# A short-conv mixer on one core: product b of a chunk's two pairs by seven products of half size, and buffers as 2 KB pages

## The chip, the core and the metric

The kernel runs on one core of a Trainium2 chip. The metric is the device time of one launch in microseconds (us). PE is TensorE, DVE VectorE, ACT ScalarE, POOL GpSimd, and SP the engine whose queue issues the transfers.

## The reference

With DEPTH = 1 there is one layer, the gated short convolution. Its input is 1024 tokens of width 1024, its inner width is 2048.

```python
u = rms_norm(x, pre_norm)
z, bg, cg, v = split(u @ w_in, 4, axis=-1)          # w_in: 1024 x 8192
y = bg * causal_dwconv(cg * v, conv_w) * silu(z)    # 3 taps per channel
h = x + rms_norm(y @ w_out, post_norm)              # w_out: 2048 x 1024
```

All is float32.

## The kernel before, in words

The work on `u @ w_in` goes by chunks of 128 inner channels (16 chunks) and, in each, by two pairs of 128-channel columns of `w_in`: an even pair p = 2c (cg and v) and an odd pair p = 2c+1 (z and bg). A pair is a product of a 2 x 2 block matrix (two channel columns by two halves of the model width) with a 2 x 2 block matrix of `u` (two halves of the model width by two halves of the tokens). It is done with seven block products instead of eight, named a, b, c, e, d, f, g in the order in which `ORDER` runs them. The sums of weight blocks that some of them need are made on GpSimd in `add_s`, the sums of `u` once at the start.

Each block product is 128 channels by 512 inner by 512 tokens. Every operand is split into a high part (a cast on ScalarE) and the rest (a subtraction on VectorE), in `split`; `product` then issues, for each of four inner slices of 128, three matmuls over 512 columns: low weight by high u, high weight by low u, high by high. That is 12 matmuls to a product. Products a, c, d, g accumulate in one PSUM bank (px), e and f in another (pv), b in a third (py). `after` reads a bank after each product: `snap` copies it to SBUF on ScalarE after a, c and e; after b, d and f VectorE adds the bank to the copy.

After g of an even pair the convolution follows: VectorE multiplies into `gpad`, and `conv` does the first tap on ScalarE and two more on VectorE, each over all 1024 tokens. After g of the odd pair the chunk is gated, and its y is written to DRAM (`y_done`).

The engines run their queues in the order in which the code issues, since the schedule is by hand. Between products the loop over p puts in the work for later pairs: `split_w` and `add_s` for pair p+1, `fetch` of the weights of pair p+2 on SP, and sums for the output stage (`fetch_t`, `add_t` on `w_out`; `fetch_s`, `add_y` on y). The first chunk (pair 0 plain, pair 1 in seven products) is mixed with the norm and the transposes of x. The output stage multiplies y by `w_out` with seven block products too (`out_mm`), its operands fetched and split a unit at a time (`fetch_unit`, `split_unit`), and ends with the norm and the residual.

Buffers come from several pools: `raw` (16 KB tiles: weights of a pair, sums, fetched units), `wp` (8 and 4 KB tiles: split weights), `snp`, `tmp`.

Of the kernel before, what the change touches and what calls it, by code (L numbers as in the profile page):

```python
# [14 lines left out]
WARM = 14  # L15


@with_exitstack
def kernel(
# [16 lines left out]
    nc = tc.nc  # L36
# [22 lines left out]
    wp = ctx.enter_context(tc.tile_pool(name="wp", bufs=3))  # L59
    raw = ctx.enter_context(tc.tile_pool(name="raw", bufs=3))  # L60
# [5 lines left out]
    def bank(name):  # L66
        return psum.tile([P, HB], F32, tag="bank", name=name)

# [42 lines left out]
    raws, sums, wt = {}, {}, {}  # L111

    def fetch(p, rows=(0, 1)):
        if p >= len(PAIRS):
            return
        c, tys = PAIRS[p]
        if p not in raws:
            raws[p] = raw.tile([P, 2, NK, P], F32, tag="raw", name=f"raw_{p}")
        for n in rows:
            c0 = tys[n] * CI + c * P  # L120
            nc.sync.dma_start(raws[p][:, n], wiv[:, :, c0 : c0 + P])

    def add_s(p, part):

        if p >= len(PAIRS):
            return
        r = raws[p]
        a11, a12, a21, a22 = (flat(r[:, n, k * KH : (k + 1) * KH]) for n in (0, 1) for k in (0, 1))
        if part == 0:
            sums[p] = raw.tile([P, 4, HB], F32, tag="sum", name=f"sum_{p}", bufs=1)  # L130
        s = sums[p]
        if part == 0:
            nc.gpsimd.tensor_add(s[:, 1], a21, a22)  # L133
            nc.gpsimd.tensor_sub(s[:, 0], s[:, 1], a11)
        else:
            nc.gpsimd.tensor_sub(s[:, 2], a11, a21)  # L136
            nc.gpsimd.tensor_sub(s[:, 3], a12, s[:, 0])  # L137
# [5 lines left out]
    def split_w(p, part):  # L143

        if p >= len(PAIRS):
            return
        n = 2 * HB if part < 3 else HB
        tag = "w8" if part < 3 else "w4"
        if p == 1 and part == 1:
            t = raw.tile([P, 2, n], F32R, tag="raw", name=f"w{part}_{p}")  # L150
        else:
            t = wp.tile([P, 2, n], F32R, tag=tag, name=f"w{part}_{p}", bufs=3 if part < 3 else 2)
        if part == 0:
            src = flat(raws[p][:, 0])
        elif part == 3:
            src = flat(raws[p][:, 1, KH:])
        else:
            src = flat(sums[p][:, 2 * (part - 1) : 2 * part])
        split(src, t[:, 0], t[:, 1])
        wt[p, part] = t  # L160


    WHERE = {"a": (0, 0), "b": (0, HB), "c": (1, 0), "e": (1, HB), "d": (2, 0), "f": (2, HB), "g": (3, 0)}
# [12 lines left out]
    def product(p, i, ks=None):  # L176

        part, off = WHERE[i]
        w = wt[p, part]
# [5 lines left out]
        for k in range(KH) if ks is None else ks:  # L185
            hi = w[:, 0, off + k * P : off + (k + 1) * P]
            lo = w[:, 1, off + k * P : off + (k + 1) * P]
            last = k == KH - 1
            nc.tensor.matmul(ps, lo, UH[i][:, k], start=first and k == 0, stop=False, skip_group_check=True)  # L189
            nc.tensor.matmul(ps, hi, UL[i][:, k], start=False, stop=False, skip_group_check=True)  # L190
            nc.tensor.matmul(ps, hi, UH[i][:, k], start=False, stop=last, skip_group_check=True)  # L191
# [3 lines left out]
    def snap(p, i):  # L195
        t = snp.tile([P, HB], F32, tag="sn", name=f"sn{i}_{p}", bufs=5)
        nc.scalar.copy(t, banks[p, "v" if i == "e" else "x"])
        sn[p, i] = t
# [5 lines left out]
    def after(p, i):  # L204
# [9 lines left out]
        elif i == "c" and p % 2:  # L214
            nc.scalar.activation(sn[p, "a"], sn[p, "a"], AF.Silu)
# [13 lines left out]
        elif i == "g":  # L229
# [5 lines left out]
            else:  # L235
                nc.vector.tensor_mul(gpad[:, TAPS - 1 : TAPS - 1 + HB], x_, sn[p, "a"])
                conv(c)
# [8 lines left out]
    def fetch_s(c):  # L246

        if c >= CH:
            done[c] = done[c], raw.tile([P, 4, HB], F32, tag="raw", name=f"s_{c}")
            nc.sync.dma_start(flat(done[c][1][:, :2]), y_d[:, c - CH])  # L250

    def add_y(c):

        if c < CH:
            cv = done.pop(c)
            t = tmp.tile([P, HB], F32, tag="s3", name=f"s3_{c}")
            nc.vector.tensor_sub(t, cv[:, :HB], cv[:, HB:])
            nc.sync.dma_start(s_d[:, SK["d"], c], t)
        else:
            cv, t = done.pop(c)  # L260
            nc.vector.tensor_add(t[:, 1], t[:, 1], cv[:, HB:])
            nc.vector.tensor_sub(t[:, 0], t[:, 1], t[:, 0])
            nc.vector.tensor_sub(t[:, 2], cv[:, :HB], t[:, 0])
            nc.sync.dma_start(s_d[:, :3, c - CH], t[:, :3])
# [3 lines left out]
    def fetch_t(j):  # L268
        ts[j] = raw.tile([P, 4, HB], F32, tag="raw", name=f"t_{j}")
        nc.sync.dma_start(ts[j].rearrange("p (k e) d -> p k (e d)", k=2), wov[:, j :: CH])  # L270

    def add_t(j, eng):

        t = ts.pop(j)
        eng.tensor_sub(t[:, 1], t[:, 1], t[:, 0])
        eng.tensor_sub(t[:, 3], t[:, 3], t[:, 1])
        eng.tensor_sub(t[:, 0], t[:, 3], t[:, 0])
        eng.tensor_sub(t[:, 2], t[:, 2], t[:, 3])
        nc.sync.dma_start(t_d[:, :, j], t)
# [8 lines left out]
    snp = mixed.enter_context(tc.tile_pool(name="snp", bufs=1, reuse_waits="tile"))  # L288
# [8 lines left out]
    rows = wp.tile([P, 2 + TH, P], F32, tag="w4", name="rows", bufs=2)  # L297
    grow, cw_rows = rows[:NK, 0], rows[: TAPS * NC, 1]
    junk = wp.tile([P, D], F32, tag="w4", name="junk", bufs=2)
    sq = small.tile([P, NT], F32, tag="sq", name="sq", bufs=1)  # L300
    gcol = small.tile([P, NK], F32, tag="gcol", name="gcol", bufs=1)
    dg = rows[:, 2:]
# [7 lines left out]
    raws[0] = raw.tile([P, 2, NK, P], F32, tag="raw", name="raw_0")  # L310
# [9 lines left out]
    def square(t):  # L320

        out = flat(raws[0][:, 0]) if t == 0 else junk
# [43 lines left out]
    def high_plain(p, n):  # L366
        plain_w[p, n] = wp.tile([P, 2, D], F32R, tag="w8", name=f"wn{n}_{p}", bufs=3)
        nc.scalar.copy(plain_w[p, n][:, 0], flat(raws[p][:, n]))

    def low_plain(p, n):  # L370
        t = plain_w[p, n]
        nc.vector.tensor_sub(t[:, 1], flat(raws[p][:, n]), t[:, 0].bitcast(F32))

    def plain(p, n, half, part, kks=range(4), first=None, last=None):
# [4 lines left out]
        ps, w = banks[p, n, half], plain_w[p, n]  # L379
        first = part == 0 if first is None else first  # L380
        last = part == 1 if last is None else last
        for j, kk in enumerate(kks):
            k = part * KH + kk
            hi, lo = (w[:, h, k * P : (k + 1) * P] for h in (0, 1))
# [5 lines left out]
    def plain_snap(p, n):  # L390
        t = snp.tile([P, HB], F32, tag="sn", name=f"sp{n}_{p}", bufs=5)
# [15 lines left out]
    for t in range(TH):  # L407
        square(t)
        if t == 0:
# [5 lines left out]
            fetch(2)  # L415
# [25 lines left out]
    low_plain(0, 1)  # L441
    for k in range(KH):
# [15 lines left out]
    split_w(1, 0)  # L458
# [11 lines left out]
    add_s(1, 0)  # L470
    rebuild(0, [2, 3])
    add_s(1, 1)
# [31 lines left out]
    sn[1, "a"] = snp.tile([P, HB], F32, tag="sn", name="sna_1", bufs=5)  # L504
# [13 lines left out]
    split_w(1, 1)  # L518
# [27 lines left out]
    split_w(1, 2)  # L546
# [8 lines left out]
    split_w(1, 3)  # L555
# [4 lines left out]
    split_w(2, 0)  # L560
# [8 lines left out]
    add_s(2, 0)  # L569
    add_s(2, 1)  # L570
    fetch(3)

    def conv(c):
        cv = tmp.tile([P, L], F32, tag="cv", name=f"cv_{c}", bufs=2)
# [7 lines left out]
    def first_chunk(i):  # L582

        if i == "":
# [4 lines left out]
            split_w(2, 1)  # L589
            conv(0)  # L590
            nc.gpsimd.tensor_mul(cvs[0][:, HB:], cvs[0][:, HB:], sn[1, "e"])
        elif i == "a":
            split_w(2, 2)
        elif i == "b":
            split_w(2, 3)
# [5 lines left out]
        elif i == "d":  # L601
# [3 lines left out]
            y_done(0, cv)  # L605

# [7 lines left out]
    def fetch_unit():  # L614
# [12 lines left out]
        tag, bufs = ("sum", 1) if n % 4 == 3 else ("raw", 3)  # L627
        r = raw.tile([P, CQ, HB], F32, tag=tag, name=f"r{side}_{i}{h}", bufs=bufs)
        nc.sync.dma_start(r, src)
        fetched.append(r)  # L630

    def split_unit():
# [5 lines left out]
        for q in (slice(0, CQ // 2), slice(CQ // 2, CQ)):  # L638
            split(flat(fetched[n][:, q]), flat(t[:, 0, q]), flat(t[:, 1, q]))
# [4 lines left out]
    TODO[2 * CH + 1] = CH - 1  # L644
    first_chunk("")
    for p in range(2, len(PAIRS)):
        q, prev = p + 1, p // 2 - 1
        for i in ORDER:
            product(p, i)
            after(p, i)  # L650
            if p == 2:
                first_chunk(i)
            if i == "a" and p < END:
                add_s(q, 0)
                if p in TODO:
                    fetch_t(TODO[p])
                if p % 2 == 0 and p > 2:
                    fetch_s(prev)
                if p + 2 <= END:
                    fetch(p + 2)  # L660
            if p == END - 1 and i in "cd":
                fetch_unit()
            if p == END:
                if i in "abcdg":
                    split_unit()
                    fetch_unit()
            elif i == "b":
                split_w(q, 0)
                add_s(q, 1)
                if p in TODO:  # L670
                    add_t(TODO[p], nc.gpsimd if p % 2 else nc.vector)
                if p == 3 or p % 2 == 0 and p > 2:
                    add_y(prev)
            elif i == ("e" if p > 2 else "d"):
                split_w(q, 1)
            elif i == "f":
                split_w(q, 2)
            elif i == "g":
                split_w(q, 3)
# [9 lines left out]
    gpost = wp.tile([P, D], F32, tag="w4", name="gpost", bufs=2)  # L689
    nc.sync.dma_start(gpost, post_norm.broadcast_to([P, D]))  # L690
    xr = wp.tile([P, 2, D], F32, tag="w8", name="xr", bufs=3)
    gx = wp.tile([P, TH, HB], F32, tag="w8", name="gx", bufs=3)
    acc = p2.tile([P, 3, TH, HB], F32, tag="acc", name="acc")
    jk = p2.tile([P, HB], BF16, tag="jk", name="jk")
    so = small.tile([P, NT, NE], F32, tag="so", name="so", bufs=1)
    C11, C12, C22 = (acc[:, j] for j in range(3))
# [14 lines left out]
    def halves_of(t):  # L711
        q = t % TH
        return (C11[:, q], C12[:, q]) if t < TH else (ob["x", q], C22[:, q])
# [115 lines left out]
```

## Time and profile before

| | us |
|---|---|
| median of 3 runs | 792.23 (791.69 to 792.39) |
| the profiled execution | 791.43 |
| its span, first to last instruction | 789.6 |
| PE busy in the span | 781.3 (99%) |
| DVE busy | 532.2 (67%) |
| ACT busy | 309.3 (39%) |
| POOL busy | 293.4 (37%) |

In rows of operations the form is: start, length, engine, line, operation, output<-inputs, size, count, and in brackets the idle time before and what ended it. In rows of groups: line, engine, operation, names, size, count, then busy us and mean ns, then the idle time before. A row that gives one line's instructions has the shortest, median and longest duration in ns. In rows of windows: the stretch, its length, then busy us and count for PE, weight loads (PEld), DVE, ACT and POOL (or for POOL alone), the granted clock, the transfers' share and GB/s.

### The profile page before, as it was taken

The page shows a single profiled execution, that of the slowest core. Times are in us where ns is not written, and L with a number is a line of the kernel's source. Part 1 is how long each engine was busy: PE and PEld are TensorE (multiplying, and loading weights), DVE is VectorE, ACT ScalarE, POOL GpSimd, SP SyncE. Part 2 cuts the span into 40 slices and gives each one's busy share as a digit, 9 for nine tenths or more (in the row PEclk, how much of TensorE's full clock was granted, in tenths as well). Part 3 has the DMA queues.
Part 4 walks back from the last instruction along what each step waited for, and adds up shares of the span by engine and source line. Part 5 has one row for each costly group of instructions (what it writes and reads, how often), then busy time and mean ns, then how long its engine had stood idle before and what let it go on. Part 6 is the DMA issues. An engine that isn't in the chain of part 4 may idle for free.

```text
span 789.6 us, 9038 instructions
## 1 busy us (share of the span) xinstructions
PE 781.3 (99%) x3494; PEld 647.9 (82%) x3494; DVE 532.2 (67%) x578; ACT 309.3 (39%) x425; POOL 293.4 (37%) x197
## 2 busy tenths in 40 slices
PE   9999999999999999999999999999999999999996
PEld 8888888888888888888888888888888888888885
DVE  6799676767676767586666666666666857633766
ACT  8555423333333333332333232333332636544441
POOL 2618644444444444456444444434443100000020
PEclk9999999999999999999999999999999999999999
DMA  9130370707061625246232414141505569455237
GB/s 319 56 99 8 94 238 16 253 1 253 26 228 43 212 67 187 93 164 207 95 127 75 147 54 148 53 148 52 180 22 198 215 233 415 180 198 213 107 110 263
DMA packets 94282, 114.38 MB, mean 145 GB/s; under 512 B 2920, under 2 KB 68512, under 8 KB 92192
## 3 DMA queue, kind: packets, MB, share of 16 engines
q1 hardware_dynamic: 94224, 113.81, 42.4%
q8 instruction: 27, 0.44, 0.2%
q14 instruction: 15, 0.12, 0.0%
q10 hardware_dynamic: 16, 0.00, 0.0%
HBM read 84.44 MB, written 29.36 MB: 144 GB/s over the span
## 4 chain that ended last, share of the span: by engine, by line
PE 98%; DVE 0%; DMA 0%; ACT 0%; issue 0%; DVEq 0%
PE px L189 14%; PE px L190 14%; PE px L191 14%; PE pv L189 7%; PE pv L191 7%; PE pv L190 7%; PE po_x L708 4%; PE po_x L709 4%; PE po_x L707 4%; PE py L189 4%; PE py L191 4%; PE py L190 4%; PE po_v L708 2%; PE po_v L709 2%; PE po_v L707 2%; PE pp L388 1%
## 5 line engine op out<-in xcount | busy, mean ns | idle before, releaser
L141 DVE TENSOR_TENSOR w<-sum,w 128x1024 fp32r<-128x1024 f32 x62 | 93.7, 1511 | 77.3 <-ACT w L140 77.3
L141 DVE TENSOR_TENSOR w<-raw,w 128x1024 fp32r<-128x1024 f32 (+1 forms) x62 | 98.3, 1587 | 5.2 <-ACT w L140 5.2
L140 ACT CAST w<-sum 128x1024 fp32r<-128x1024 f32 x62 | 65.0, 1049 | 63.1 <-issue 54.5
L577 DVE SCALAR_TENSOR_TENSOR cv<-gpad,cw,cv 128x1024 f32<-128x1024 f32 x32 | 63.7, 1989 | 20.2 <-ACT cv L575 19.6
L140 ACT CAST w<-raw 128x1024 fp32r<-128x1024 f32 (+1 forms) x62 | 51.5, 833 | 59.9 <-PE py L191 59.9
L228 POOL TENSOR_TENSOR gpad<-snc,sne 128x512 f32<-128x512 f32 x15 | 20.4, 1360 | 138.9 <-DVE snc L223 138.9
L136 POOL TENSOR_TENSOR sum<-raw 128x512 f32<-128x512 f32 x31 | 61.0, 1969 | 0.0
L220 POOL TENSOR_TENSOR sne<-sne,cv 128x512 f32<-128x512 f32 x15 | 20.4, 1363 | 100.6 <-DVE sne L218 85.2
L223 DVE TENSOR_TENSOR snc<-pv,snc 128x512 f32<-128x512 f32 x30 | 20.7, 691 | 54.3 <-PE pv L191 54.3
L747 POOL TENSOR_TENSOR acc<-acc,xr 128x512 f32<-128x512 f32 x4 | 6.9, 1719 | 133.1 <-DVE acc L746 133.1
L137 POOL TENSOR_TENSOR sum<-raw,sum 128x512 f32<-128x512 f32 x31 | 54.6, 1763 | 0.0
L133 POOL TENSOR_TENSOR sum<-raw 128x512 f32<-128x512 f32 x31 | 41.5, 1337 | 31.4 <-DVE w L141 31.4
L189 PE MATMUL py<-u_b,w 128*128 128x512 f32 x124 | 48.4, 391 | 0.0
L189 PE MATMUL px<-u_a,w 128*128 128x512 f32 x124 | 48.3, 390 | 0.0
L191 PE MATMUL py<-u_b,w 128*128 128x512 f32 x124 | 48.2, 389 | 0.0
L190 PE MATMUL py<-u_b,w 128*128 128x512 f32 x124 | 48.2, 389 | 0.0
L191 PE MATMUL px<-u_a,w 128*128 128x512 f32 x124 | 48.2, 389 | 0.0
L190 PE MATMUL px<-u_a,w 128*128 128x512 f32 x124 | 48.2, 389 | 0.0
L189 PE MATMUL px<-u_c,w 128*128 128x512 f32 x124 | 48.2, 389 | 0.0
L190 PE MATMUL px<-u_c,w 128*128 128x512 f32 x124 | 48.2, 389 | 0.0
L191 PE MATMUL px<-u_c,w 128*128 128x512 f32 x124 | 48.2, 389 | 0.0
L189 PE MATMUL pv<-u_e,w 128*128 128x512 f32 x124 | 48.2, 389 | 0.0
(259 smaller groups left out, 2073.7 us busy)
## 6 DMA issues: line engine op xcount, KB each, us to landing
raw<-in_sc_w_in SPq DMA_DIRECT2D x64, 512.0 KB, 5.4
y_d<-cv SPq DMA_DIRECT2D x16, 512.0 KB, 3.2
t<-in_sc_w_out SPq DMA_DIRECT2D x8, 1024.0 KB, 5.9
t_d<-t SPq DMA_DIRECT2D x8, 1024.0 KB, 4.3
s_d<-s SPq DMA_DIRECT2D x8, 768.0 KB, 3.6
s<-y_d SPq DMA_DIRECT2D x8, 512.0 KB, 4.5
xr<-in_x SPq DMA_DIRECT2D x8, 512.0 KB, 4.5
out<-acc SPq DMA_DIRECT2D x12, 256.0 KB, 2.5
```

The costliest lines, as they stand in the source:

```text
L133: nc.gpsimd.tensor_add(s[:, 1], a21, a22)
L136: nc.gpsimd.tensor_sub(s[:, 2], a11, a21)
L137: nc.gpsimd.tensor_sub(s[:, 3], a12, s[:, 0])
L140: nc.scalar.copy(hi, src)
L141: nc.vector.tensor_sub(lo, src, hi.bitcast(F32))
L189: nc.tensor.matmul(ps, lo, UH[i][:, k], start=first and k == 0, stop=False, skip_group_check=True)
L190: nc.tensor.matmul(ps, hi, UL[i][:, k], start=False, stop=False, skip_group_check=True)
L191: nc.tensor.matmul(ps, hi, UH[i][:, k], start=False, stop=last, skip_group_check=True)
L577: nc.vector.scalar_tensor_tensor(cv, gpad[:, j : j + L], tap(c, j), cv, op0=ALU.mult, op1=ALU.add)
L707: nc.tensor.matmul(ps, lo, u[:, 0, k], start=first, stop=False, skip_group_check=True)
L708: nc.tensor.matmul(ps, hi, u[:, 1, k], start=False, stop=False, skip_group_check=True)
L709: nc.tensor.matmul(ps, hi, u[:, 0, k], start=False, stop=last, skip_group_check=True)
```

## The change

From the third chunk on (`DEEP = 2`), product b is no longer done for each pair by itself. The two pairs of a chunk take the same `u` block in it, so their four blocks (two pairs by two halves of the inner 512) form a 2 x 2 block matrix again, and the `u` block of 512 by 512 another. Seven products of half the size (128 channels, inner 256, 256 tokens) replace the two: a', b', c', d', e', f', g'. Each has 2 inner slices by 3 matmuls over 256 columns.

```diff
+    def deep_product(c, i):
+        n, off = DEEP_W[i]
+        which = {"b'": "y'", "e'": "v'", "f'": "v'"}.get(i, "x'")
+        first = i in ("a'", "b'", "e'")
...
+        ps = banks[c, which][:, :HH]
+        for k in range(KQ):
...
+            nc.tensor.matmul(ps, lo, uh, start=first and k == 0, stop=False, skip_group_check=True)
+            nc.tensor.matmul(ps, hi, ul, start=False, stop=False, skip_group_check=True)
+            nc.tensor.matmul(ps, hi, uh, start=False, stop=k == KQ - 1, skip_group_check=True)
...
+    DEEP_C = {"a'": ("x'", 0, 0), "b'": ("y'", 0, 0), "c'": ("x'", 0, 1), "f'": ("v'", 0, 1),
+              "e'": ("v'", 1, 1), "d'": ("x'", 1, 1), "g'": ("x'", 1, 0)}
+
+    def deep_after(c, i):
+        which, row, half = DEEP_C[i]
+        t = sn[2 * c + row, "a"][:, half * HH : (half + 1) * HH]
+        nc.vector.tensor_add(t, banks[c, which][:, :HH], t)
+        if i == "f'":
+            start_conv(c)
```

`deep_after` adds the bank after each small product into half of the copy of a, and starts the convolution (`start_conv`: the multiply into `gpad`, then `conv`) after f', in the odd pair; before, it started after g of the even pair.

The sums of the weight blocks are made in each chunk on GpSimd (`deep_sums`, four operations over 256 columns), their high and low parts by `deep_prep`. The sums of the `u` block are made once: `deep_parts` on GpSimd after f of pair 2, `deep_split` (high and low parts) after g of pair 2 and after c and e of pair 3.

```diff
+    def deep_parts():
+        for k in range(KH):
+            deep[k] = page(f"deep{k}")
+            nc.gpsimd.tensor_add(deep[k], UH["b"][:, k].bitcast(F32), UL["b"][:, k].bitcast(F32))
+        for k in range(KQ):
+            (b11, b12), (b21, b22) = ((t[:, :HH], t[:, HH:]) for t in (deep[k], deep[k + KQ]))
+            nc.gpsimd.tensor_sub(b12, b12, b11)
+            nc.gpsimd.tensor_sub(b22, b22, b12)
+            nc.gpsimd.tensor_sub(b11, b22, b11)
+            nc.gpsimd.tensor_sub(b21, b21, b22)
```

The order of the products is now a list of slots. In an even pair from the third chunk on it is c, a', e, b', d, f, c', a of the next pair, e', g; in an odd one c, f', e, d', d, g', f, a of the next pair, g. Weights are split when the slot that needs them is less than 7 us away by a table of 2.72 us for a product and 0.72 for a small one:

```diff
+        sub = {"c": "a'", "e": "b'", "f": "c'", "a": "e'"} if p % 2 == 0 else {"c": "f'", "e": "d'", "d": "g'"}
...
+    def prepare(n):
+        while ready[0] < len(slots) and at[ready[0]] < at[n + 1] + LEAD:
+            i, p = slots[ready[0]]
+            if i[1:]:
+                deep_prep(p, i)
+            elif (p, i) not in wt:
+                split_w(p, i)
+            ready[0] += 1
+
+    first_chunk("")
+    for n, (i, p) in enumerate(slots):
+        if i[1:]:
+            deep_product(p, i)
+            prepare(n)
+            deep_after(p, i)
+            if i == "g'":
+                nc.scalar.activation(sn[2 * p + 1, "a"], sn[2 * p + 1, "a"], AF.Silu)
+            continue
+        product(p, i)
+        prepare(n)
+        after(p, i)
...
+        if i == "c":
...
+            if p % 2 == 0 and p // 2 >= DEEP:
+                deep_sums(p // 2, 1)
+        elif i == "e":
+            add_s(q, "ec")
+        elif i == "d":
+            if p + 2 <= END:
+                fetch(p + 2)
+            add_s(q, "d")
...
+        elif i == "f":
+            add_s(q, "f")
...
+            if p == 2 and DEEP < NC:
+                deep_parts()
+        elif i == "g":
+            if p in TODO:
+                add_t(TODO[p], nc.gpsimd if p % 2 else nc.vector)
+            if p % 2 and q <= END and q // 2 >= DEEP:
+                deep_sums(q // 2, 0)
+            if p == 2 and DEEP < NC:
+                deep_split("c'")
+                deep_split("e'")
...
+        if p == END and i in "acdg":
+            split_unit()
+            fetch_unit()
```

The pools `raw`, `wp`, `snp` give way to one pool of 36 pages of 2 KB a partition. What was one operation over 1024 columns (a cast or a subtraction in `split`) or one transfer of a large tile becomes two to four over 512 columns, one per page. The buffer of the convolution (`cv`) has one copy instead of two.

More of the change, by code (lines that the diff above doesn't have):

```diff
@@ L141, in split, with split_w @@
         nc.vector.tensor_sub(lo, src, hi.bitcast(F32))
-    def split_w(p, part):
+    def split_w(p, kinds):
         if p >= len(PAIRS):
             return
[L147 to L163, printed above, removed]
+        for i in kinds:
+            hi, lo = (page(f"w{i}{h}_{p}", F32R) for h in "hl")
+            split(block(p, *BLOCK[i]) if i in BLOCK else sums[p, i], hi, lo)
+            wt[p, i] = hi, lo
     ORDER = "abcedfg"
@@ L320, in square @@
     def square(t):
[L322 removed]
+        out = block(0, 0, 0).bitcast(BF16) if t == 0 else junk
         nc.scalar.activation(out, xs[t], AF.Square, scale=D ** -0.5, accum_out=sq[:, t : t + 1])
@@ new lines, with deep_split @@
+    DEEP_U = {"c'": (KQ, HH), "d'": (0, 0), "g'": (KQ, 0), "e'": (0, HH)}
+    def deep_split(i):
+        k0, l0 = DEEP_U[i]
+        ls = slice(l0, l0 + HH)
+        if i != "e'":
+            deep[i] = [tmp.tile([P, KQ, HH], F32R, tag="ub", name=f"u{i[0]}{h}_deep", bufs=6) for h in "hl"]
+        for k in range(KQ):
+            if i == "e'":
+                hi, lo = UH["b"][:, k, ls], UL["b"][:, k, ls]
+            else:
+                hi, lo = (t[:, k] for t in deep[i])
+            split(deep[k0 + k][:, ls], hi, lo)
@@ new lines, in deep_sums @@
+    def deep_sums(c, part):
+        (a11, a12), (a21, a22) = ((t[:, :HH], t[:, HH:]) for t in (block(p, 0, 1) for p in (2 * c, 2 * c + 1)))
+        t = page(f"ds{part}_{c}")
+        deep[c, part] = t
+        if part == 0:
+            nc.gpsimd.tensor_add(t[:, :HH], a21, a22)
+            nc.gpsimd.tensor_sub(t[:, HH:], t[:, :HH], a11)
+        else:
+            nc.gpsimd.tensor_sub(t[:, :HH], a11, a21)
+            nc.gpsimd.tensor_sub(t[:, HH:], a12, deep[c, 0][:, HH:])
+    DEEP_W = {"a'": (0, 0), "b'": (0, HH), "e'": (1, 0), "c'": (1, HH), "d'": (2, 0), "f'": (2, HH), "g'": (3, 0)}
@@ L626, in fetch_unit @@
             src = plain_y[i] if i in plain_y else s_d[:, SK[i], js]
-        tag, bufs = ("sum", 1) if n % 4 == 3 else ("raw", 3)
-        r = raw.tile([P, CQ, HB], F32, tag=tag, name=f"r{side}_{i}{h}", bufs=bufs)
-        nc.sync.dma_start(r, src)
+        r = [page(f"r{side}_{i}{h}{k}") for k in range(CQ)]
+        for k in range(CQ):
+            nc.sync.dma_start(r[k], src[:, k])
         fetched.append(r)
@@ new lines @@
+    slots = [("a", 2), ("b", 2)]
+    for p in range(2, len(PAIRS)):
+        q = p + 1
+        more = p // 2 >= DEEP
+        sub = {"c": "a'", "e": "b'", "f": "c'", "a": "e'"} if p % 2 == 0 else {"c": "f'", "e": "d'", "d": "g'"}
+        for i in "cedf":
+            slots.append((i, p))
+            if more and i in sub:
+                slots.append((sub[i], p // 2))
+        if q <= END:
+            slots.append(("a", q))
+            if more and p % 2 == 0:
+                slots.append((sub["a"], p // 2))
+            if q // 2 < DEEP:
+                slots.append(("b", q))
+        slots.append(("g", p))
```

282 lines of the change are left out of this document (155 added, 127 removed).

## The prediction

> **What bounds the kernel now.** I read the page first (engines, then the chain that ended last), then the windows by stage, then the rows of single operations.
>
> ```profile
> span 789.6 us, 9038 instructions
> ...
> PE 781.3 (99%) x3494; PEld 647.9 (82%) x3494; DVE 532.2 (67%) x578; ACT 309.3 (39%) x425; POOL 293.4 (37%) x197
> PE 98%; DVE 0%; DMA 0%; ACT 0%; issue 0%; DVEq 0%
> ...
> 80.00:630.00 550.00, 550.00 (x2428) 455.40 (x2428) 371.44 (x338) 192.58 (x252) 246.31 (x160) 1.00 0.39 129
> ```
>
> The last row is the main loop: TensorE (PE, the first number after the length) is busy 550.00 of 550.00 us at a granted clock of 1.00, VectorE (DVE) 371 us, ScalarE (ACT) 193, GpSimd (POOL) 246. PE alone ends the chain, so two things count: what the products cost, and whether PE now has to wait. The profiled execution took 791.4 us, 1.8 more than its span and 0.8 less than the median of 792.2; I sum against 791.4.
>
> **The products.** Each chunk from the third on (14 of 16) loses two products of 12 matmuls over 512 columns and gets seven of 6 over 256.
>
> ```profile
> 299.68 0.39 PE L190 MATMUL px<-u_d,w 128*128 128x512 f32 x1
> ...
> 302.86 0.39 PE L189 MATMUL pv<-u_f,w 128*128 128x512 f32 x1
> L190 PEld LDWEIGHTS py<-u_b,w 128*128 128x128 f32 x124 | 23.3, 188 | 4.8
> 10.74 1.95 PE L342 MATMUL pk<-rows,xa 128*128 128x128 f32 x16
> L342 PE MATMUL pk<-rows,xa 128*128 128x128 f32 x48 | 6.2, 279 | 0.6 <-DVE rows L417 0.6
> 25.79 0.50 PE L189 MATMUL py<-u_b,w 128*128 128x512 f32 x1
> 26.13 0.39 PE L190 MATMUL py<-u_b,w 128*128 128x512 f32 x1
> ```
>
> Fourteen starts from 299.68 to 302.86 make 0.227 us for a 512-column matmul, 2.72 us a product. No 256-column matmul is in the trace. From below: half of 0.227 is 0.113, and the pieces of the plain f32 matmuls at L342 (24 calls, 48 records), each with a weight load of its own, follow each other every (1.95-0.28)/15 = 0.111 us. So a load can be had every 0.111 us. From above: a load is shown as 188 ns; if the next matmul had to wait for all of it, a step would be 0.188. I take 0.115, nearest to the rows that are measured as a rate; a part of the 512's step may not halve. Then a chunk pays 42 x 0.115 = 4.83 us for 24 x 0.227 = 5.44: 0.61 us saved, 8.5 us over 14 chunks (10.9 at 0.111; a loss of 34 at 0.188).
>
> [...]
>
> **The new wait.** All four x' products of a chunk (a', c', d', g') accumulate in one bank, and `deep_after` adds the bank to a buffer on VectorE after each. So g' may not write before VectorE has read what d' left. PE reaches g' soon: the order is c, f', e, d', d, g'. In VectorE's order there stand ahead of that read: the low half of f's weights (the lead of 7 us puts its split just behind f'), the add after f', the whole convolution (`start_conv` now follows f'), and a weight split. The rows:
>
> ```profile
> 314.87 0.39 PE L191 MATMUL px<-u_c,w 128*128 128x512 f32 x1
> 315.30 0.59 ACT L197 COPY snc<-px 128x512 f32<-128x512 f32 x1 [1.62 <-PE px L191]
> L140 ACT CAST w<-raw 128x512 fp32r<-128x512 f32 x31 | 18.9, 610 | 0.0
> L141 DVE TENSOR_TENSOR w<-raw,w x62: 687/1702/2315, 22.6 to 616.6; 128x1024 fp32r<-128x1024 f32 x31, 128x512 fp32r<-128x512 f32 x31
> 8.74 0.17 DVE L427 COPY gcol<-pw 128x8 f32<-128x8 f32 x1 [0.79 <-PE pw L425]
> L223 DVE TENSOR_TENSOR snc<-pv,snc 128x512 f32<-128x512 f32 x30 | 20.7, 691 | 54.3 <-PE pv L191 54.3
> 305.55 2.02 DVE L141 TENSOR_TENSOR w<-sum,w 128x1024 fp32r<-128x1024 f32 x1 [0.44 <-ACT w L140]
> 307.49 0.68 DVE L236 TENSOR_TENSOR gpad<-px,sna 128x512 f32<-128x512 f32 x1
> 308.25 1.16 ACT L575 ACTIVATE cv<-gpad,cw 128x1024 f32<-128x1024 f32 x1 [2.74 <-DVE gpad L236]
> 309.44 4.20 DVE L577 SCALAR_TENSOR_TENSOR cv<-gpad,cw,cv 128x1024 f32<-128x1024 f32 x2 [1.27 <-ACT cv L575]
> L577 DVE SCALAR_TENSOR_TENSOR cv<-gpad,cw,cv x32: 1285/1967/2309, 63.7 to 615.4; 128x1024 f32<-128x1024 f32 x32
> ```
>
> Clock from the recorded end of c (zero; the first two rows give 0.04 us to ScalarE). Snap of c 0.59, to 0.63. f's cast stands behind it on ScalarE, starts some 0.05 before that ends and takes 0.61: 1.19. f's low half on VectorE: 0.03 of handoff and 0.69 (the least of L141): 1.91. Back-to-back operations of VectorE overlap by 0.08 (305.55+2.02 against 307.49). The 256-wide add after f': not in the trace, between 0.17 (8 columns) and 0.69 (512), in proportion 0.42: 2.25. The gpad multiply 0.68: 2.85. ScalarE's tap, 0.08 later, 1.16: 4.09. Two more taps on VectorE, 0.03 later, at their least 1.285 each: 6.62. The split of the next a, 0.69: 7.23. The add after d', 0.42: 7.57. PE starts 0.04 later, and the first matmul after a wait takes 0.11 longer (0.50 against 0.39 in the two rows at 25.79): 7.72.
>
> PE without a wait: its next product starts 0.39-0.227 = 0.16 before c's recorded end; f', d' at 0.69 and e, d at 2.72 make 6.82, so g' is due at 6.66. PE waits 1.06 us, in each of the 14 chunks, more than the 0.61 saved. Behind it on PE queue f, a and all that follows; nothing else runs on PE meanwhile.
>
> Bounds: with the two adds at 0.17 the wait is 0.56, at 0.69 1.6. With the taps at the median of L577, 1.967 beside GpSimd, 1.4 more: 2.5. I take the least durations, because GpSimd should be quiet then: before the convolution it has only the sums e and c of the next pair, two operations of some 1.3 us, and then its queue stops at the multiply that waits for VectorE's add after d. 1.06 x 13 chunks = 13.8 us. In the last chunk `split_unit` puts four casts of 0.61-0.05 ahead of f's cast: 1.06+2.2 = 3.3.
>
> **Once, ahead of the third chunk.** `deep_parts` puts four 512-wide adds and eight half-wide ones on GpSimd after product f of pair 2, and `deep_split` puts casts that wait for them on ScalarE, ahead of f's cast and of the snap of c of pair 3, for which product d waits.
>
> ```profile
> 57.40:88.70 31.30, 28.44 (x16) 1.00 0.26 75
> L403 POOL TENSOR_TENSOR xa<-u_a x4: 1282/1294/1300, 13.6 to 30.1; 128x512 f32<-128x512 f32 x4
> ```
>
> In that stretch 15 operations (and a memset of 0.1) took GpSimd 28.44 us, 1.89 each; alone one takes 1.29. From the end of f: VectorE's add 0.69, gpad multiply, f's sum, four adds and six half adds worth nine operations, 17.0 us (11.6 at 1.29); then on ScalarE three half casts, a cast and the snap, 2.2: 19.9 (14.5). PE has a, b, g, c, e until d: 13.6. It waits 6.3 us (0.9). I take 6, since VectorE is as loaded there as in the row.
>
> **The rest.** VectorE gains per chunk 1.5 splits (1.0), seven small adds for two big ones (1.6) and two short operations for each long one (about 1): 25.7 us of a chunk's 38.1 (371.44 of 550) become some 29 of 38.5, no bound. Transfers get smaller and more on SP, the fetches, `add_y` and `add_t` stand some products later, and each transfer waits in SP's order for the last reader of its buffer:
>
> ```profile
> raw<-in_sc_w_in SPq DMA_DIRECT2D x64, 512.0 KB, 5.4
> ```
>
> A pair's weights are asked for after d and summed after e of the next pair, 4 x 2.72 + 3 x 0.69 = 13 us later, where 5.4 us bring them. A buffer that frees late eats up to 7.5 us of that before anyone notices. Without this cover a late block would hold GpSimd's sums, then the splits. For that, for VectorE's backlog in the third chunk and for GpSimd's four t operations ahead of chunk 9, I put 2 us (0 to 6). Output stage and tail keep their matmuls: nothing.
>
> Sum: 791.4 - 8.5 + 13.8 + 3.3 + 6 + 2 = 808.0, and 0.8 to the median: **809 us**.
>
> **Rivals.**
> *The wait is not there (faster).* If the chain from c to the add after d' is 1.06 us shorter, and setup finds GpSimd at 1.29, it is 792.2 - 8.5 + 1 + 2 = 787. It decides at 6.66 us after c. For it: two of the steps (the 256-wide adds) are in no row, and at 0.17 each half of it is gone. Against: the other eight are taken at their least already. 13%.
> *Same.* A wait of 0.3 each and setup at 1: 792.2 - 8.5 + 14 x 0.3 + 4 = 792. 4%.
> *The taps meet GpSimd (slower still).* Late weights shift its two sums into the convolution; the wait is 2.5: 792.2 - 8.5 + 14 x 2.5 + 2.2 + 6 + 2 = 829. For it: the median of L577; against: the quiet argued above. 12%. [...]
> *The weight load bounds (0.188).* f' and d' last 1.13, so the wait falls to 0.2, but the products lose 34: 792.2 + 34 + 14 x 0.2 + 2.2 + 6 + 2 = 839. Against: 0.111 at L342. 5%.
>
> **How the numbers follow.** The forecast has 66%. The range runs from 787 to 829, the centres of the faster case and of the loud taps: it leaves out about half of each (6 and 6%) and the weight load's 5%, some 17 in 100. About 0.2% (1.6 us) is what can be told from no change. Faster 0.13, same 0.04, slower 0.83.
>
> **What would show it.** In the trace after: 256-column starts 0.111 to 0.12 apart; PE idle of about 1 us before the last product of each chunk (`deep_product`, released by VectorE's add after d'), 14 times; one idle of some 6 us near 90 to 100 us, ended by ScalarE's snap; PE short of 100% in the loop. No such idle, or steps over 0.13, would make the prediction wrong.

## The result, and the profile after

The changed kernel takes 818.1 us (median of 5 runs, 816.38 to 820.32), the kernel before 792.1 (5 runs, 791.69 to 792.39): a ratio of 1.033, 95% interval 1.0318 to 1.0341. It is slower by 26 us; the forecast was 17 us slower. The profiled execution took 817.24 us, 25.8 more than that of before. In order of the page: the engines, the chain that ended last, two windows, and TensorE's waits.

```profile
span 815.3 us, 10812 instructions
...
PE 785.2 (96%) x3746; PEld 655.8 (80%) x3746; DVE 645.3 (79%) x835; ACT 333.1 (41%) x612; POOL 356.8 (44%) x265
...
PE 62%; DVE 16%; issue 7%; ACT 5%; DMA 5%; POOL 4%; SPq 1%; DVEq 0%; POOLq 0%; ACTq 0%
```

```profile
89.50:102.30 12.80, 6.08 (x17) 4.48 (x16) 8.42 (x12) 6.21 (x15) 9.61 (x10) 0.73 0.00 0
102.30:655.90 553.60, 538.54 (x2630) 451.40 (x2629) 463.32 (x518) 201.54 (x363) 296.87 (x214) 1.00 0.38 123
```

```profile
PE px L684 <- DVE sna L695: 15.1, 14, 3.3
PE px L188 <- ACT snc L196: 6.7, 1, 6.7
PE pw L324 <- DVE idle L290: 1.1, 1, 1.1
```

TensorE ended 98% of the chain before and ends 62% of it now; VectorE has come in with 16%. In the second window PE is idle 15 us of 553.6, and the waits say where: 14 times at L684, the first matmul of a small product, until VectorE's add at L695. That is the wait of g' for the add after d'. One more, of 6.7 us, stands in the first window, where the granted clock is 0.73 too.

The starts of TensorE's matmuls give the ledger of the 25.8 us. A step's excess is taken against the steps of before, 0.227 us for 512 columns:

| | us | forecast |
|---|---|---|
| small products, 588 matmuls of 256 columns, and the matmuls behind them | -4.1 | -8.5 |
| the 14 waits before g', with the slower first matmul behind each | +18.8 | +17.1 |
| the wait ahead of product d of pair 3 | +7.2 | +6 |
| the matmuls behind that wait, at a lower clock | +2.1 | none |
| the rest (0.5 at the head, 0.3 at 65 us, 0.2 at 392 us, 0.8 in single steps and the tail) | +1.8 | +2 |

### The profile page after: what moved, and what is told of

It reads as the page before. It is cut to its first block, busy times and chain, and to the rows that moved or that the text cites. A ratio compares the mean times of both kernels' runs of the same rounds, so it can differ in the third digit from the quotient of the medians.

```text
span 815.3 us, 10812 instructions
## 1 busy us (share of the span) xinstructions
PE 785.2 (96%) x3746; PEld 655.8 (80%) x3746; DVE 645.3 (79%) x835; ACT 333.1 (41%) x612; POOL 356.8 (44%) x265
## 4 chain that ended last, share of the span: by engine, by line
PE 62%; DVE 16%; issue 7%; ACT 5%; DMA 5%; POOL 4%; SPq 1%; DVEq 0%; POOLq 0%; ACTq 0%
PE px L188 9%; PE px L189 9%; PE px L190 9%; PE pv L188 4%; PE pv L189 4%; PE pv L190 4%; PE po_x L858 3%; PE po_x L859 3%; PE po_x L857 3%; DVE cv L583 2%; PE po_v L858 2%; PE po_v L859 2%; PE po_v L857 2%; PE px L684 1%; ACT cv L581 1%
## 5 line engine op out<-in xcount | busy, mean ns | idle before, releaser
L583 DVE SCALAR_TENSOR_TENSOR cv<-gpad,cw,cv 128x1024 f32<-128x1024 f32 x32 | 42.0, 1313 | 19.0 <-ACT cv L581 18.4
L188 PE MATMUL px<-u_d,wdl 128*128 128x512 f32 x124 | 49.7, 401 | 6.7 <-ACT snc L196 6.7
L150 POOL TENSOR_TENSOR sf<-raw,sc 128x512 f32<-128x512 f32 x31 | 53.5, 1725 | 0.0
L155 DVE TENSOR_TENSOR wel<-se,weh 128x512 fp32r<-128x512 f32 x31 | 52.9, 1706 | 0.0
L146 POOL TENSOR_TENSOR se<-raw,raw 128x512 f32<-128x512 f32 x31 | 52.0, 1677 | 0.9 <-ACT sna L196 0.5
L148 POOL TENSOR_TENSOR sc<-se,raw 128x512 f32<-128x512 f32 x31 | 49.7, 1602 | 3.0 <-POOL se L146 0.7
L189 PE MATMUL px<-u_d,wdh 128*128 128x512 f32 x124 | 49.5, 399 | 0.0
L190 PE MATMUL px<-u_d,wdh 128*128 128x512 f32 x124 | 49.0, 395 | 0.0
L188 PE MATMUL pv<-u_e,wel 128*128 128x512 f32 x124 | 48.6, 392 | 0.0
L189 PE MATMUL pv<-u_e,weh 128*128 128x512 f32 x124 | 48.6, 392 | 0.0
L188 PE MATMUL pv<-u_f,wfl 128*128 128x512 f32 x124 | 48.6, 392 | 0.0
L188 PE MATMUL px<-u_a,wal 128*128 128x512 f32 x124 | 48.5, 391 | 0.0
```

What stands on the lines that cost most here:

```text
L146: nc.gpsimd.tensor_add(t, block(p, 1, 0), block(p, 1, 1))
L148: nc.gpsimd.tensor_sub(t, sums[p, "e"], block(p, 0, 0))
L150: nc.gpsimd.tensor_sub(t, block(p, 0, 1), sums[p, "c"])
L155: nc.vector.tensor_sub(lo, src, hi.bitcast(F32))
L583: nc.vector.scalar_tensor_tensor(cv, gpad[:, j : j + L], tap(c, j), cv, op0=ALU.mult, op1=ALU.add)
```

## The experiments

Times are medians beside runs of the kernel before on the same chip (791.9 us each time), the ratio with its 95% interval.

**1. The convolution behind d'.**

```diff
-        if i == "f'":
+        if i == "d'":
             start_conv(c)
```

> The changed kernel with one step moved: the convolution (the multiply into gpad, then the three taps) is queued behind VectorE's add after d' instead of behind the one after f'. Nothing is computed otherwise. My theory: g' waits only because the convolution stands ahead of the add after d' on VectorE. The 14 waits before g' (17.3 us beyond the usual gap) go, the start after d' stays at the usual 0.23 to 0.35 us, and the time falls from 818.1 to about 801. Rival one: VectorE is loaded to 79% and is late by its total work; then the wait comes back at another product of the chunk and the time stays within 2 us of 818. Rival two: only the part up to the cast of f's weights is late (some 1.2 us of chain before any VectorE work), and half the wait stays: about 810.

809.48 us (809.01 to 810.34), ratio 1.0224 (1.0207 to 1.0241). TensorE's waits in it, then four operations of ScalarE in one chunk and the matmul that waited for the last of them:

```profile
PE px L188 <- ACT snc L196: 6.7, 1, 6.7
PE px L188 <- ACT sna L196: 6.1, 13, 0.5
PE pv L188 <- ACT sne L196: 1.7, 1, 1.7
...
296.42 0.63 ACT L779 ACTIVATE sna<-sna 128x512 f32<-128x512 f32 x1 [3.76 <-DVE sna L695]
296.96 0.60 ACT L154 CAST wch<-sc 128x512 fp32r<-128x512 f32 x1
299.81 0.63 ACT L222 ACTIVATE snc<-snc 128x512 f32<-128x512 f32 x1 [2.25 <-DVE snc L220]
301.38 0.57 ACT L196 COPY sna<-px 128x512 f32<-128x512 f32 x1
302.01 0.50 PE L188 MATMUL px<-u_c,wcl 128*128 128x512 f32 x1 [0.47 <-ACT sna L196]
```

No wait at L684 is left: the order of VectorE's queue made it, as the theory said. But 8.6 us went and not 17. The time is that of rival two (about 810), though half a wait at g' is not what is left; rival one is half right, since a wait has come back at another product, and only experiment 6 decides whether VectorE's load makes it. It came 13 times, at product c of the next even pair, 0.63 us beyond the usual gap plus 0.11 for the first matmul. Its way is in the rows: the SiLU of z stands in ScalarE's queue behind g' and waits 3.76 us for the add after g', which the convolution now holds up; the cast of c's weights stands behind it, then VectorE's split and its add after f, the SiLU that waits for that (299.81), two casts, and only then the copy of product a, for which product c waits. One more wait, of 1.7 us, stands before product f ahead of chunk 9, where GpSimd does the four sums of `w_out` (380.6 to 387.5 us). And some 0.75 us of the gain is not the move's: the setup's wait is the same 6.9 us, but six slow steps follow it here instead of ten.

**2. The casts of the u sums later.** `deep_split` for c' behind d of pair 3 (not g of pair 2), for e' and d' behind f, for g' behind g.

```diff
-            if p == 2 and DEEP < NC:
-                deep_split("c'")
-                deep_split("e'")
         if p == 3 and DEEP < NC:
-            if i == "c":
-                deep_split("d'")
-            elif i == "e":
-                deep_split("g'")
+            if i == "d":
+                deep_split("c'")
+            elif i == "f":
+                deep_split("e'")
+                deep_split("d'")
+            elif i == "g":
+                deep_split("g'")
```

> The changed kernel with the casts of the sums of the u block moved to later products of pair 3: those for c' behind d, those for e' and d' behind f, those for g' behind g; nothing is cast any more behind g of pair 2 and behind c and e of pair 3. Nothing is computed otherwise. My theory: product d of pair 3 no longer waits (the 6.9 us idle at 90 us goes) and, as TensorE no longer stands still, the ten or so matmuls that started 0.427 us apart behind that wait start 0.227 apart again, with the granted clock back at 1.00: together 9.2 us less, about 809. Rival one: GpSimd itself is late, so the wait comes back at c' or a' of the third chunk: less than 3 us gained. Rival two: the slow matmuls came from something else that starts there (the first sums of the third chunk): 6.9 us gained and the matmuls still 0.427 apart, about 811.

815.50 us (813.84 to 816.85), ratio 1.0296 (1.0277 to 1.0315): 2.6 us gained by the medians and 0.5 by the profiled executions (816.78 against 817.24), so rival one. The wait has moved from product d of pair 3 to product c of pair 4:

```profile
106.30 0.79 PE L188 MATMUL px<-u_c,wcl 128*128 128x512 f32 x1 [5.12 <-ACT sna L196]
```

What holds ScalarE there is the cast of c's weights of pair 4, which waits for GpSimd's sum, behind the twelve operations of `deep_parts` (82.3 to 97.8 us in this trace). So the casts were the place where GpSimd's 15 us were felt, more than the cause; experiment 7, where those sums are spread and the wait is gone, bears this out. The slow steps moved with the wait: twelve starts after it are 0.427 us apart again. They come once more in the last chunk (0.214 and 0.427 us), which costs another 1.5 us in this trace; its granted clock is 0.992 over the span, where the changed kernel has 0.994.

**3. Both.** The two edits above in one kernel.

> Both moves at once: the convolution behind d', and the casts of the sums of the u block behind d, f and g of pair 3. Nothing is computed otherwise. My theory, by which the two waits are separate and all that is lost: 818.1 - 17.3 - 9.2 = 791.6, so level with the kernel before (792.1) within 1.5 us, since the smaller products themselves save only 2 to 3 us net. If the products saved what I forecast (8.5 us), and something else hides it, nothing else would be seen idle and the time would be 786. If the waits hide one another, the gain is less than the sum of the two single moves: above 796.

808.29 us (808.09 to 808.63), ratio 1.0206 (1.0191 to 1.0221). Against the kernel with the first move it gains 1.2 us: both waits had come back elsewhere, so my 791.6 was out by 17. The two gains add up to 11.2 (8.6 + 2.6), against 9.8 here; the 1.4 between them is less than the 3 us by which experiment 2's runs differ among themselves, so that the waits hide one another is not shown. Each move passes most of its wait on.

**4. The pages alone.** No small product at all.

```diff
-DEEP = 2
+DEEP = 16
```

> The changed kernel with no smaller products at all (the first chunk to use them is set past the last), so that only the pages, the smaller transfers and the new way to time the splits are left of the change. Nothing is computed otherwise than in the kernel before. My theory: the pages cost TensorE next to nothing, 0 to 1 us: 792 to 793. Rival: late buffers and more, smaller transfers cost the 2 us that I put for them or more: 794 to 798, with idle time of TensorE in the loop.

793.26 us (792.88 to 793.76), ratio 1.0017 (1.0008 to 1.0027): 1.35 us. From its page and its weight loads' waits:

```profile
PE 783.2 (99%) x3494; PEld 647.9 (82%) x3494; DVE 508.1 (64%) x729; ACT 319.4 (40%) x576; POOL 279.8 (35%) x197
PEld pv L188 <- issue: 1.7, 7, 0.2
```

TensorE is as full as before. The starts lie 0.48 us later from 12 us on, another 0.37 at 65 us, and 0.12 in each of seven chunks, where product f comes just behind its low weights. That is small, but a third of what the products turn out to save. The 0.48 need not be the pages': it begins where ScalarE waits for a transfer of x at 7 to 8 us, the trace of experiment 5, a kernel without pages, has it too (0.47), and those of experiments 6 and 8, with pages, hardly do (0.07 and 0.04).

**5. The price of 256 columns alone.** The kernel before, product b in two halves of its columns from pair 4 on.

```diff
+            cuts = (slice(0, HB // 2), slice(HB // 2, HB)) if i == "b" and p >= 4 else (slice(0, HB),)
+            for ls in cuts:
+                nc.tensor.matmul(ps[:, ls], lo, UH[i][:, k, ls], start=first and k == 0, stop=False, ...)
...
```

Both halves lie in one bank and both begin with a start. The output lies 0.17 (relative error) from the reference, so the sum of product b is not whole in this kernel; which part of it is left out, no run shows. Its instructions are all there, and only their time is read.

> The kernel before, with product b of every pair from the third chunk on issued in two halves of its columns: for each slice of weights three matmuls over the first 256 columns, then three over the last 256, so 24 matmuls of 256 columns where 12 of 512 stood, and no other work changed. It measures the price of a 256-column matmul alone, without the waits. My theory now (starts 0.1187 us apart, as in the changed kernel, and later 512-column matmuls a little slowed): 28 products x (24 x 0.1187 - 2.72) = 3.6 us more, and some 0.8 for the matmuls behind: 792 + 4.4 = 796. The forecast's step of 0.115: 28 x 0.04 = 1.1 more, 793. The lower bound of 0.111: 1.6 less, 790.5.

797.66 us (796.84 to 798.20), ratio 1.0074 (1.0060 to 1.0088): 5.8 us more. First, second and last matmul of such a product, and the three behind it:

```profile
100.70 0.28 PE L191 MATMUL py<-u_b,w 128*128 128x256 f32 x1
100.82 0.28 PE L192 MATMUL py<-u_b,w 128*128 128x256 f32 x1
...
103.46 0.28 PE L193 MATMUL py<-u_b,w 128*128 128x256 f32 x1
103.58 0.40 PE L191 MATMUL px<-u_c,w 128*128 128x512 f32 x1
103.81 0.40 PE L192 MATMUL px<-u_c,w 128*128 128x512 f32 x1
104.05 0.39 PE L193 MATMUL px<-u_c,w 128*128 128x512 f32 x1
```

24 matmuls take 2.87 us (103.58 less 100.70): 0.1197 a step, with no wait in it, where 12 of 512 columns take 2.72. And the next five steps of 512 columns are 0.228 to 0.236 instead of 0.227, together 0.027 us more. So 28 x (2.87 - 2.72 + 0.03) = 5.0 us by the trace. Its profiled execution has another 0.47 us at the head, ahead of any halved product (see experiment 4). Only the first step of a product is half of 0.227 (0.113); the others are 0.119 to 0.120, which decides against 0.115 and 0.111.

**6. ScalarE's copy of a ahead of the casts, and the SiLU of z behind that copy.** Experiment 3, and:

```diff
-            if i == "g'":
+            if i == "g'" and p == NC - 1:
                 nc.scalar.activation(sn[2 * p + 1, "a"], sn[2 * p + 1, "a"], AF.Silu)
...
         product(p, i)
-        prepare(n)
-        after(p, i)
+        if i == "a" and p % 2 == 0:
+            after(p, i)
+            if p // 2 > DEEP:
+                nc.scalar.activation(sn[p - 1, "a"], sn[p - 1, "a"], AF.Silu)
+            prepare(n)
+        else:
+            prepare(n)
+            after(p, i)
```

> As the kernel with both moves (convolution behind d', casts of the u sums later), and on ScalarE the copy of product a of each even pair is queued ahead of the casts for the next products, and the SiLU of z behind that copy instead of behind g'. Nothing is computed otherwise. There, product c of each even pair still waited 0.63 us beyond the usual gap, 13 times, for that copy: the SiLU held ScalarE until VectorE's add after g', behind the convolution, and the cast, split, add after f, SiLU and two more casts came before the copy. My theory: the wait is the order of ScalarE's queue, and 8 us go: about 800. Rival: it is the convolution's length on VectorE that arrives here; half of the wait or more stays: 804 or above.

796.18 us (795.83 to 796.98), ratio 1.0060 (1.0044 to 1.0075). 12.1 us went, more than the 8 of the theory: the 13 waits (8.1 us, 1.4 of their first matmuls) are all gone, and the setup wait, which ended with the same copy in pair 4, fell from 5.3 to 3.9 us, and the granted clock is 0.996 over the span where experiment 3 had 0.994. Another 0.5 us went at the wait before product f ahead of chunk 9, and 0.5 at the head, which differs from trace to trace. So the 13 waits were the order of ScalarE's queue, and not VectorE's load, which is 80% here too. Two operations were moved in that queue; which of them was needed was not tested.

**7. No wait in the loop.** Experiment 6; the small products begin with the fourth chunk (`DEEP = 3`), and the chunk ahead of them is used for the sums of u. The `TODO` line puts all sums of `w_out` on VectorE, behind even pairs.

```diff
-DEEP = 2
+DEEP = 3
...
-    TODO = {p: p // 2 - 2 for p in range(4, 4 + 2 * CH - 2, 2)}
-    TODO[2 * CH + 1] = CH - 1
+    TODO = {p: p // 2 - 3 for p in range(6, 6 + 2 * CH, 2)}
...
+        if p == 4 or (p == 3 and i in "dfg"):
+            next(deep_work, None)
+        sp = {("f", 4): "c'", ("e", 5): "d'", ("f", 5): "g'", ("e", 6): "e'"}.get((i, p))
+        if sp:
+            deep_split(sp)
...
```

> As the kernel before this one in the list, and the sums of the u block spread over the chunk ahead, for which the smaller products start one chunk later (from the fourth on): one or two GpSimd operations behind each product of pairs 3 and 4, the casts behind four products of pairs 4 to 6; and the sums of w_out, once done on GpSimd ahead of chunk 9, all on VectorE in even pairs from pair 6 on. Nothing is computed otherwise. My theory: no wait of TensorE is left in the loop. What stays is the smaller products' own gain, 13 x (5.44 - 4.95 for the seven - about 0.2 by which the matmuls behind them are slowed) = 3.8 us, against 1.35 for the pages: 791.9 + 1.35 - 3.8 = 789.5, so a little faster than the kernel before. Rival: VectorE's and GpSimd's extra work comes back as waits wherever it is put; 793 or above. If the products saved the forecast 0.61 us a chunk in full, 785.

791.78 us (791.30 to 792.35), ratio 0.9999 (0.9990 to 1.0008): level with the kernel before. The setup wait is gone and the granted clock is 0.998 over the span, as before. Six gaps are left (0.3, 0.5, 0.3, 0.3, 0.3 us at 407 to 447 us, 0.4 at 627), 2.1 of the 2.3 us that it lies above my 789.5.

**8. Those six.** Against experiment 7, the last sum of `w_out` goes from pair 20 to pair 24, and the first unit of the output stage is split behind a, d, f and g of the last pair.

```diff
-    TODO = {p: p // 2 - 3 for p in range(6, 6 + 2 * CH, 2)}
+    TODO = {**{p: p // 2 - 3 for p in range(6, 20, 2)}, 24: 7}
...
-        if p == END and i in "acdg":
+        if p == END and i in "adfg":
```

> As the version with no wait aimed for in the loop (small products from the fourth chunk on, sums of u spread, copy of a ahead of the casts), and the last of the sums of w_out moved on VectorE from behind g of pair 20 to behind g of pair 24, away from the sums of y that begin there, and in the last chunk the first unit of the output stage is split behind a, d, f and g instead of a, c, d and g. Nothing is computed otherwise. Left in that version beyond the usual gaps were 0.2 (407 us), 0.48, 0.32, 0.26, 0.18 (426 to 447 us) and 0.44 us (627 us). My theory: VectorE's four extra operations caused those at 426 to 447 us and the unit's casts that at 627: 1.2 to 1.7 us less than 791.8, about 790.3, so 0.2% faster than the kernel before. Rival: the sums of y are what is too much there; the waits stay and the time is 791.8 again, no difference from the kernel before.

789.59 us (789.39 to 789.84), ratio 0.9972 (0.9961 to 0.9983): 0.28% faster than the kernel before, and 28.5 us faster than the changed kernel, with the same small products in all chunks but one. Its page and its waits:

```profile
span 787.5 us, 10772 instructions
...
PE 778.2 (99%) x3728; PEld 653.5 (83%) x3728; DVE 631.2 (80%) x832; ACT 334.0 (42%) x610; POOL 346.7 (44%) x257
...
PE 90%; DVE 4%; DMA 2%; ACT 1%; issue 1%; SPq 0%; POOL 0%; DVEq 0%; ACTq 0%
PE pw L324 <- DVE idle L290: 1.1, 1, 1.1
PE pk L348 <- DVE dg L423: 0.9, 1, 0.9
PE pv L188 <- DVE wel L155: 0.2, 1, 0.2
```

Two of the three waits stand at the head, before any product. PE is busy 3.1 us less than before: 546 matmuls of 256 columns take 64.6 us by their starts and slow the others by 2.4, where 312 of 512 took 70.7, so about 3.8 us saved, 0.29 in each of 13 chunks. That is what the idea is worth in this kernel where nothing waits. In this trace 1.2 us of it goes into four short gaps (68, 407, 516 and 521 us), each with its slower first matmul.

## Why the prediction was right, and where its sum was off

The direction, the cause and the place were right, and 818.1 lies in the range (787 to 829); its sum was 9.2 us short of the profiled difference. Step by step:

**The wait of g'.** This is the chain that was worked out, in one chunk: on TensorE the end of c, f', the last of d and g'; on ScalarE the copy of c and f's cast; on VectorE f's low half, the add after f', the multiply into `gpad`, the two taps, the split of a, the add after d'.

```profile
287.89 0.39 PE L190 MATMUL px<-u_c,wch 128*128 128x512 f32 x1
288.12 0.28 PE L684 MATMUL pv<-u_b,dw2l 128*128 128x256 f32 x1
...
294.80 0.39 PE L190 MATMUL px<-u_d,wdh 128*128 128x512 f32 x1
296.03 0.39 PE L684 MATMUL px<-ugh_deep,dw 128*128 128x256 f32 x1 [0.85 <-DVE sna L695]
288.31 0.59 ACT L196 COPY snc<-px 128x512 f32<-128x512 f32 x1 [4.77 <-PE px L190]
288.80 0.62 ACT L154 CAST wfh<-sf 128x512 fp32r<-128x512 f32 x1
289.45 0.69 DVE L155 TENSOR_TENSOR wfl<-sf,wfh 128x512 fp32r<-128x512 f32 x1 [0.67 <-ACT wfh L154]
290.06 0.42 DVE L695 TENSOR_TENSOR sna<-pv,sna 128x256 f32<-128x256 f32 x1
290.51 0.69 DVE L236 TENSOR_TENSOR gpad<-px,sna 128x512 f32<-128x512 f32 x1
292.43 2.61 DVE L583 SCALAR_TENSOR_TENSOR cv<-gpad,cw,cv 128x1024 f32<-128x1024 f32 x2 [1.22 <-ACT cv L581]
294.95 0.68 DVE L155 TENSOR_TENSOR wal<-raw,wah 128x512 fp32r<-128x512 f32 x1
295.56 0.42 DVE L695 TENSOR_TENSOR sna<-px,sna 128x256 f32<-128x256 f32 x1
```

From c's recorded end (288.28) the add after f' ends at 2.20 (forecast 2.25), the taps at 6.76 (6.62), the add after d' at 7.70 (7.57), and g' starts at 7.75 where it was due at 6.75 (294.80 + 0.227). The wait is 1.01 us and 0.10 for the first matmul, against 1.06. The 256-wide add, which no row of before had, is the 0.42 taken in proportion. The taps were quiet, the point on which the slower rival hung:

```profile
L583 DVE SCALAR_TENSOR_TENSOR cv<-gpad,cw,cv 128x1024 f32<-128x1024 f32 x32 | 42.0, 1313 | 19.0 <-ACT cv L581 18.4
```

1313 ns on the mean where they took 1989 before. In the chunk above GpSimd is idle all through the two (292.43 to 295.04 us); beside the two of before at 309.44 to 313.64 it was busy through all 4.20 us. Twelve chunks of 14 show 1.01. In the last the four casts of `split_unit` make 3.4 (3.3 forecast). In chunk 9 it is 1.8: by the rows GpSimd's four t operations push its sums and VectorE's splits back, which I had put into the rest; no run tests this alone. Experiment 1 shows the cause, and shows what the prediction did not ask: what is late next, if this wait goes.

**The setup.** The wait came where it was put, and somewhat longer: 6.9 us beyond the usual gap and 0.4 for the first matmul.

```profile
76.39 0.39 PE L190 MATMUL pv<-u_f,wfh 128*128 128x512 f32 x1
78.33 0.68 DVE L220 TENSOR_TENSOR snc<-pv,snc 128x512 f32<-128x512 f32 x1
82.42 6.96 POOL L618 TENSOR_TENSOR deep<-u_b 128x512 f32<-128x512 f32 x4
...
94.27 0.72 POOL L622 TENSOR_TENSOR deep<-deep,deep 128x256 f32<-128x256 f32 x1
95.02 0.40 ACT L154 CAST uch_deep<-deep 128x256 fp32r<-128x256 f32 x1 [2.74 <-POOL deep L622]
95.33 0.71 ACT L154 CAST u_b<-deep 128x256 fp32r<-128x256 f32 x2
95.94 0.61 ACT L154 CAST wfh<-sf 128x512 fp32r<-128x512 f32 x1
96.47 0.57 ACT L196 COPY snc<-px 128x512 f32<-128x512 f32 x1
97.09 0.79 PE L188 MATMUL px<-u_d,wdl 128*128 128x512 f32 x1 [6.71 <-ACT snc L196]
97.68 0.63 PE L189 MATMUL px<-u_d,wdh 128*128 128x512 f32 x1
98.11 0.63 PE L190 MATMUL px<-u_d,wdh 128*128 128x512 f32 x1
```

The four adds take 1.74 us each, as feared beside a loaded VectorE (busy 5.38 of these 6.96 us), and the copy of c stands last on ScalarE behind casts that wait for them. The chain from the end of f (76.78) to the end of that copy (97.04) is 20.3 us where 19.9 were forecast, but this is partly luck, since two terms were off against each other: VectorE's add after f ends 2.2 us after f and not 0.69, as it stands behind other work, and GpSimd, from its multiply at 79.09 to the subtraction that ends at 94.99, takes 15.9 us and not 17.0. What the step missed lies in the last two rows: the starts behind the wait are 0.43 us apart and not 0.227. Ten such steps, and one of 0.33, cost 2.1 us more.

**The products: the term that failed.** Their saving was put at 0.61 us a chunk, 8.5 in all; it is 4.1 here. Two things were off, in this kernel's starts and in experiment 5 alike. A step takes 0.118 on the mean (0.115 for the first of a product, then 0.118 to 0.119), not the 0.115 that I chose between 0.111 and 0.188: 588 x 0.003 = 1.8 us. I had leaned on the f32 matmuls of 128 columns (0.111 apart), which showed how fast weights can follow one another, not what a 256-column step costs. And the matmuls behind a small product start 0.228 to 0.236 apart for five steps: 2.6 us that no row of before could show. So 4.4 of the 9.2 us by which the sum fell short lie here; 2.1 are the clock, 1.7 the waits, 1.2 the setup's wait, less 0.2 of the rest.

**The rest.** 1.8 us beside 2, so the size was right, but not for the reasons given. The 0.5 at the head need not come from the change (experiment 4), 0.3 at 65 us comes with the pages (it is in experiment 4 too), and the 0.12 a chunk that the pages cost alone is not seen here. In the loop, buffers and transfers cost nothing that a wait shows. VectorE became busier than forecast, 84% of the second window (463.32 of 553.60) where 29 of 38.5 us make 75%; it set no bound even so.

**The rivals.** *The wait is not there* and *the same* fell with the 14 waits. *The weight load bounds* fell with the step of 0.118. *The taps meet GpSimd* gave a time almost as near as the forecast's (829 against 818, where 809 was forecast) for a reason that did not occur. So the time came out above the forecast by smaller items, none of which was a rival.

## What to carry to other kernels

When an operation is queued ahead of another on an engine that runs its queue in order, as ScalarE does in experiment 1 (a wait of 3.76 us), walk the chain past the first wait: take it away on paper and ask what is late next, since here two moves that removed their waits entirely (g', setup) gave back half or more of the gain at a later product, and only the moves of experiments 6 to 8 got it out. A long piece of one-time work on a side engine is best spread over a stretch that has room, not shifted as a block. And fewer columns in more matmuls must be priced by their own step, and by what the matmuls behind them lose, before the rest of a schedule is built on the saving: here 0.29 us of an expected 0.61 per chunk.

## What the runs showed of the hardware that I had not expected

**The clock after an idle stretch.** After 6.9 us of idle TensorE, ten steps of 512 columns take 0.427 us each, 4.3 us in all, and the granted clock of the window is 0.73. After 5.3 us, in experiment 2, it is eleven, and two of 256 columns at 0.214. After an excess of 3.4 us before g' of the last chunk it is one or the other:

```profile
649.60 0.39 PE L684 MATMUL px<-ugh_deep,dw 128*128 128x256 f32 x1 [3.25 <-DVE sna L695]
649.82 0.28 PE L685 MATMUL px<-ugl_deep,dw 128*128 128x256 f32 x1
```

This is the changed kernel; in experiment 2 the same wait is followed by steps of 0.21:

```profile
648.03 0.58 PE L684 MATMUL px<-ugh_deep,dw 128*128 128x256 f32 x1 [3.24 <-DVE sna L695]
648.41 0.41 PE L685 MATMUL px<-ugl_deep,dw 128*128 128x256 f32 x1
```

In the changed kernel the granted clock is 0.50 from 95.32 to 102.15 us, 1.00 from there to 812.12, behind the last product, and 0.50 after that. So it fell 4.9 us after the last recorded end ahead of the wait (90.38) and rose 5.1 us after the first matmul behind it (97.09): the slow steps are the part of these 6.83 us that lies behind the wait. At the wait before g' of the last chunk it stayed at 1.00 here (640 to 656 us). How long TensorE has to be idle for such a fall, and what sets its moment, these runs do not show; they show that the same wait can end in different ways. The same 6.9 us before product d are followed by ten slow steps here and by six in experiment 1, and the same 3.25 us before g' by slow steps in one execution and by none in the other. Such a wait so costs up to almost half more than itself (2.4 on 5.3 us in experiment 2).

**512 columns behind 256.** The five steps behind a product of 256-column matmuls are 0.232, 0.235, 0.229, 0.232 and 0.231 on the mean in the changed kernel and within some 0.001 of that in experiment 5, then 0.227 again. What is caught up there, and why a 256-column step takes 0.120 and not 0.114, these runs leave open; no experiment took the weight loads away.
